# DRAM blocks of 17 and 15 rows per partition, and turns of rows to match them, in a fused residual-add layer normalisation

## The chip, the cores and the metric

The kernel runs on one core of a Trainium2 chip; nothing else is run beside it. The metric is the device time of one execution in microseconds (us). Each kernel is executed several times, and the medians are compared.

Names of engines as the profile has them: PE is TensorE, DVE VectorE, ACT ScalarE, POOL GpSimd, SP SyncE. SPq is SyncE's own instruction stream, from which it issues the transfers. They go into one DMA queue, which 16 DMA engines serve. A packet is one record of the DMA trace: here the rows of one partition in one transfer (16 rows are 32 KiB), or a completion of 4 bytes. A transfer has landed when its completions have arrived.

## The reference, cut to what matters

```python
batch, seq, dim = 16, 1024, 512              # x and residual, float32
z = x + residual
mean = np.mean(z, axis=-1, keepdims=True)
var = np.var(z, axis=-1, keepdims=True)
return gamma * (z - mean) / np.sqrt(var + eps) + beta
```

There are 16384 rows of 512 floats (2 KiB), 128 rows for each of the 128 partitions. 32 MiB of x and 32 MiB of residual come in, 32 MiB go out.

## The kernel before

Two buffers stay in SBUF: `zbuf` for 64 rows per partition of x, later of output, and `rbuf` for 32 rows of residual, later of the sum. SyncE alone issues all transfers of rows, in the order of a fixed plan (`x0+8` loads x rows 0 to 7, `o0+16` stores rows 0 to 15). A transfer is put into the queue when the buffer rows that it needs are free:

```python
BLOCK = 16
PLAN = """
x0+8 r0+8 x8+8 r8+8 x16+16 r16+16 x32+16 r32+16 x48+16
o0+16 r48+16 o16+16 x64+16 r64+16 x80+16 o32+16 r80+16
x96+16 r96+16 o48+8 o56+8 r112+8 x112+8 r120+8 x120+8
o64+16 o80+16 o96+16 o112+8 o120+4 o124+4
"""
TURN = 4
# ...
def dram(t, lo, n):            # a block of 16 rows is contiguous for a partition
    b0 = lo - lo % BLOCK
    v = t[P * b0 : P * (b0 + BLOCK), :].rearrange("(p j) d -> p j d", p=P)
    return v[:, lo - b0 : lo - b0 + n, :].rearrange("p a b -> p (a b)")
# ...
elif kind == "r":              # the residual rows' old contents must have been used
    if lo + n > R_ROWS:
        last = (lo + n - R_ROWS) // TURN - 1
        nc.sync.wait_ge(s_rstd[last % Z_TURNS], last // Z_TURNS + 1)
    move(part(rbuf, R_ROWS, lo, n), dram(rf, lo, n), sr[loads_r.index((lo, n))])
else:                          # a store waits for its rows
    if lo + n > seen:
        nc.sync.wait_ge(s_out, lo + n)
```

I call such a wait a **gate**. Compute goes in turns of four rows: GpSimd adds x into `rbuf` for the whole turn; ScalarE runs one pass for the means, one for the squares, and a square root; VectorE subtracts the mean and multiplies by gamma, takes the reciprocal (at which the turn's rows of `rbuf` are free), and scales and adds beta. Activations write to scrap tiles, since only their row sums are wanted:

```python
junk_m = [nc.alloc_psum_tensor(f"junk_m{i}", [P, D], FP32) for i in range(TURN)]
junk_s = [nc.alloc_psum_tensor(f"junk_s{i}", [P, D], FP32) for i in range(6 - TURN)]
junk_s += [nc.alloc_sbuf_tensor(f"junk_s{i}", [P, D], FP32) for i in range(6 - TURN, TURN)]
```

## Time and profile before

| | before |
|---|---|
| time, median of the first 6 runs | 238.26 us (238.23 to 238.43) |
| span of the profiled run (first to last instruction) | 236.7 us |
| transfers' share of 16 DMA engines' span | 99.4% |
| busiest compute engine | ScalarE, 78% |
| bytes moved for rows | 100.66 MB |

Read it from the bottom up: every engine that computes is idle for a fifth of the span or more, and the transfers for next to nothing. The prediction below shows the lines.

### The profile page before, as it was taken

To read this page: it belongs to the slowest core of one execution; us is meant where nothing else is said; L and a number is where in the kernel's file an instruction comes from. 1 tells how busy PE (TensorE), PEld (TensorE's weight loads), DVE (VectorE), ACT (ScalarE), POOL (GpSimd) and SP (SyncE) were. 2 spreads that over 40 slices of the span, in tenths; PEclk is the share of its full clock that TensorE was granted. 3 is DMA by queue.
4 is the path that set the end of the run, shared out by engine and by line. 5 is a ranking of instruction groups with operands and counts; after the bars stand their busy time and mean duration, and the time that the engine had idled before them with its cause. 6 is when DMAs were issued, how large, how long until landed. Compare 5 with 4: busy or idle time off the path is not lost.

```text
span 236.7 us, 1000 instructions
## 1 busy us (share of the span) xinstructions
PE 3.8 (2%) x4; PEld 1.2 (0%) x4; DVE 177.2 (75%) x290; ACT 183.8 (78%) x545; POOL 144.0 (61%) x36
## 2 busy tenths in 40 slices
PE   0600000000000000000000000000000000000000
PEld 0100000000000000000000000000000000000000
DVE  0001999629999999599980999809999999999950
ACT  2019997299999996999909998099999999999600
POOL 0098920999799307993079920899799798800000
DMA  8999999999999999999999999999999999999997
GB/s 310 443 426 432 426 443 443 443 443 443 410 388 443 443 443 432 426 393 432 443 443 443 443 438 421 415 421 432 429 424 435 426 432 440 439 432 443 438 390 324
DMA packets 4469, 100.68 MB, mean 425 GB/s; under 512 B 498, under 2 KB 498, under 8 KB 500
## 3 DMA queue, kind: packets, MB, share of 16 engines
q1 hardware_dynamic: 4464, 100.67, 99.4%
q14 instruction: 1, 0.01, 0.0%
q10 hardware_dynamic: 4, 0.00, 0.0%
HBM read 67.11 MB, written 33.55 MB: 425 GB/s over the span
## 4 chain that ended last, share of the span: by engine, by line
ACT 48%; DMA 35%; POOL 6%; DVE 4%; issue 1%; SPq 1%; ACTq 0%; DVEq 0%; POOLq 0%
DMA rbuf<-in_residual_dram 35%; ACT junk_s L211 25%; ACT junk_m L201 21%; POOL rbuf L178 6%; DVE zbuf L239 3%; ACT std L220 2%; DVE zbuf L253 1%; SPq L140 1%; DVE rstd L247 0%; ACTq L194 0%; DVEq L231 0%; POOLq L175 0%; ACTq L199 0%; ACTq L195 0%
## 5 line engine op out<-in xcount | busy, mean ns | idle before, releaser
L178 POOL TENSOR_TENSOR rbuf<-zbuf,rbuf 128x2048 f32<-128x2048 f32 x32 | 143.7, 4521 | 62.2 <-DMA rbuf<-in_residual_dram 60.0
L239 DVE SCALAR_TENSOR_TENSOR zbuf<-rbuf,nm,gamma_p 128x512 f32<-128x512 f32 x128 | 87.1, 743 | 47.8 <-ACT std L220 47.8
L201 ACT ACTIVATE junk_m<-rbuf 128x512 f32<-128x512 f32 x128 | 74.2, 580 | 34.0 <-POOL rbuf L178 33.7
L211 ACT ACTIVATE junk_s<-rbuf,nm 128x512 f32<-128x512 f32 x128 | 88.8, 694 | 1.0
L253 DVE SCALAR_TENSOR_TENSOR zbuf<-zbuf,rstd,beta_p 128x512 f32<-128x512 f32 x128 | 87.1, 744 | 1.1
L211 ACT ACTIVATION_READ_ACCUMULATOR junk_s<-rbuf,nm 128x1 f32 x128 | 23.9, 187 | 0.0
L201 ACT ACTIVATION_READ_ACCUMULATOR junk_m<-rbuf 128x1 f32 x128 | 23.8, 186 | 0.0
L220 ACT ACTIVATE std<-ssq,eps_t 128x4 f32<-128x4 f32 x32 | 9.5, 297 | 1.0
L247 DVE RECIPROCAL rstd<-std 128x4 f32<-128x4 f32 x32 | 5.5, 171 | 0.0
L192 ACT ACT_TABLE_LOAD x1 | 1.3, 1283 | 2.7 <-PEq L60 2.7
L131 PE MATMUL gamma_p<-gb_row,ones 1*128 1x512 f32 x2 | 2.0, 1122 | 6.6 <-DMA gb_row<-in_gamma_dram 6.6
L131 PE MATMUL beta_p<-gb_row,ones 1*128 1x512 f32 x2 | 1.9, 1056 | 0.0
L126 DVE MEMSET ones<- 1x128 f32 x1 | 0.2, 165 | 2.0 <-PEq L60 2.0
L131 PEld LDWEIGHTS beta_p<-gb_row,ones 1*128 1x128 f32 x2 | 0.7, 332 | 1.0 <-DMA gb_row<-in_beta_dram 0.5
L131 PEld LDWEIGHTS gamma_p<-gb_row,ones 1*128 1x128 f32 x2 | 0.5, 306 | 6.6 <-issue 6.6
L294 POOL MEMSET const-float32-0.0<- 128x1 f32 x1 | 0.1, 98 | 0.2 <-issue 0.2
L294 POOL MEMSET const-bfloat16-1.0<- 128x1 bf16 x1 | 0.1, 101 | 0.0
L294 POOL MEMSET const-uint8-127<- 128x1 uint8 x1 | 0.1, 101 | 0.0
L294 POOL MEMSET const-float32-1.0<- 128x1 f32 x1 | 0.1, 98 | 0.0
L127 DVE MEMSET eps_t<- 128x1 f32 x1 | 0.1, 59 | 0.0
## 6 DMA issues: line engine op xcount, KB each, us to landing
zbuf<-in_x_dram SPq DMA_DIRECT2D x6, 4096.0 KB, 28.9
rbuf<-in_residual_dram SPq DMA_DIRECT2D x6, 4096.0 KB, 21.2
out_dram<-zbuf SPq DMA_DIRECT2D x6, 4096.0 KB, 31.0
zbuf<-in_x_dram SPq DMA_DIRECT2D x4, 2048.0 KB, 14.9
rbuf<-in_residual_dram SPq DMA_DIRECT2D x4, 2048.0 KB, 14.0
out_dram<-zbuf SPq DMA_DIRECT2D x3, 2048.0 KB, 22.5
out_dram<-zbuf SPq DMA_DIRECT2D x2, 1024.0 KB, 10.0
gb_row<-in_gamma_dram ACTq DMA_DIRECT2D x1, 2.0 KB
```

The source lines that it names most:

```text
L126: nc.vector.memset(ones[:, :], 1.0).then_inc(s_const, 1)
L131: nc.tensor.matmul(dest[:, :], ones[:, :], gb_row[:, k * D : (k + 1) * D], start=True, stop=True).then_inc(s_pe, 1)
L140: i = nc.sync.dma_start(out=out, in_=in_).then_inc(s, 16)
L178: nc.gpsimd.tensor_tensor(out=z, in0=part(zbuf, Z_ROWS, lo, n), in1=z, op=ALU.add).then_inc(s_sum[lo // TURN % R_TURNS], 1)
L192: act.preload_act_table_set("sqrt_and_others")
L201: i = act.activation(out=junk_m[k][:, :], in_=part(rbuf, R_ROWS, r, 1), func=ACT.Identity, scale=-inv_d, accum_out=column(nm, r),)
L211: i = act.activation(out=junk_s[k][:, :], in_=part(rbuf, R_ROWS, r, 1), func=ACT.Square, bias=column(nm, r), accum_out=column(ssq, r),)
L220: act.activation(out=column(std, rows[0], TURN), in_=column(ssq, rows[0], TURN), func=ACT.Sqrt, bias=eps_t[:, 0:1], scale=inv_d,).then_inc ...
L239: dve.scalar_tensor_tensor(out=part(zbuf, Z_ROWS, r, 1), in0=part(rbuf, R_ROWS, r, 1), scalar=column(nm, r), in1=gamma_p[:, :], op0=ALU.ad ...
L247: dve.reciprocal(out=column(rstd, rows[0], TURN), in_=column(std, rows[0], TURN)).then_inc(s_rstd[j], 1)
L253: i = dve.scalar_tensor_tensor(out=z, in0=z, scalar=column(rstd, r), in1=beta_p[:, :], op0=ALU.mult, op1=ALU.add,)
L294: nc = _bacc.Bacc("TRN2", target_bir_lowering=False, num_devices=1)
```

## The change

The intent is a distance between partitions in DRAM (the pitch) that is no power of two: 17 rows are 34 KiB and 15 rows 30 KiB, where 16 are 32 KiB. The compute turns change along with it, so that a turn ends where a block does (4 + 4 + 4 + 5 = 17, 4 + 4 + 4 + 3 = 15). The core of the diff:

```diff
-BLOCK = 16
+BLOCKS = [17, 15]
 PLAN = """
-x0+8 r0+8 x8+8 r8+8 x16+16 r16+16 x32+16 r32+16 x48+16
-o0+16 r48+16 o16+16 x64+16 r64+16 x80+16 o32+16 r80+16
-x96+16 r96+16 o48+8 o56+8 r112+8 x112+8 r120+8 x120+8
-o64+16 o80+16 o96+16 o112+8 o120+4 o124+4
+x0+8 r0+8 x8+9 r8+9 x17+15 r17+15 x32+17 r32+17 x49+15
+o0+17 r49+15 o17+15 x64+17 r64+17 x81+15 o32+17 r81+15
+x96+17 r96+17 o49+7 o56+8 r113+7 x113+7 r120+8 x120+8
+o64+17 o81+15 o96+17 o113+7 o120+4 o124+4
 """
-ADDS = [4] * 32
-TURN = 4
+TURNS = [4, 4, 4, 5, 4, 4, 4, 3]
 ...
-        b0 = lo - lo % BLOCK
-        v = t[P * b0 : P * (b0 + BLOCK), :].rearrange("(p j) d -> p j d", p=P)
+        k = spot(blocks, lo)
+        b0, b1 = blocks[k], blocks[k + 1]
+        v = t[P * b0 : P * b1, :].rearrange("(p j) d -> p j d", p=P)
 ...
-    junk_m = [nc.alloc_psum_tensor(f"junk_m{i}", [P, D], FP32) for i in range(TURN)]
-    junk_s = [nc.alloc_psum_tensor(f"junk_s{i}", [P, D], FP32) for i in range(6 - TURN)]
+    junk_m = [nc.alloc_psum_tensor(f"junk_m{i}", [P, D], FP32) for i in range(most)]
+    junk_s = [nc.alloc_psum_tensor(f"junk_s{i}", [P, D], FP32) for i in range(6 - most)]
 ...
-                last = (lo + n - R_ROWS) // TURN - 1
+                last = spot(marks, lo + n - R_ROWS - 1)
 ...
-                nc.sync.wait_ge(s_out, lo + n)
+                seen = next(m for m in marks if m >= lo + n)
+                nc.sync.wait_ge(s_out, seen)
```

`marks` are the rows at which turns end, `blocks` those at which blocks begin, `spot` finds the turn or block of a row, and `most` is 5. What is left out follows from these (the loops of the engines run over `marks`).

More of the change, by code (lines that the diff above doesn't have):

```diff
@@ L19 @@
 PLAN = """
-x0+8 r0+8 x8+8 r8+8 x16+16 r16+16 x32+16 r32+16 x48+16
-o0+16 r48+16 o16+16 x64+16 r64+16 x80+16 o32+16 r80+16
-x96+16 r96+16 o48+8 o56+8 r112+8 x112+8 r120+8 x120+8
-o64+16 o80+16 o96+16 o112+8 o120+4 o124+4
-"""
-ADDS = [4] * 32
-TURN = 4
-R_TURNS = R_ROWS // TURN
-Z_TURNS = Z_ROWS // TURN
+x0+8 r0+8 x8+9 r8+9 x17+15 r17+15 x32+17 r32+17 x49+15
+o0+17 r49+15 o17+15 x64+17 r64+17 x81+15 o32+17 r81+15
+x96+17 r96+17 o49+7 o56+8 r113+7 x113+7 r120+8 x120+8
+o64+17 o81+15 o96+17 o113+7 o120+4 o124+4
+"""
+TURNS = [4, 4, 4, 5, 4, 4, 4, 3]
 EARLY = 2
@@ L56, with edges, spot @@
     total = N // P
+    def edges(sizes, end):
+        found, k = [0], 0
+        while found[-1] < end:
+            found.append(found[-1] + sizes[k % len(sizes)])
+            k += 1
+        assert found[-1] == end
+        return found
+    def spot(marks, row):
+        return max(k for k, m in enumerate(marks) if m <= row)
+    blocks = edges(BLOCKS, total)
+    marks = edges(TURNS, total)
+    most = max(TURNS)
+    r_turns, z_turns = spot(marks, R_ROWS), spot(marks, Z_ROWS)
+    assert marks[r_turns] == R_ROWS and marks[z_turns] == Z_ROWS
+    assert z_turns == 2 * r_turns
     tc.close()
@@ L64 @@
         kind, (lo, n) = word[0], map(int, word[1:].split("+"))
-        assert lo // BLOCK == (lo + n - 1) // BLOCK
+        assert spot(blocks, lo) == spot(blocks, lo + n - 1)
         moves.append((kind, lo, n))
@@ L88 @@
     beta_p = nc.alloc_psum_tensor("beta_p", [P, D], FP32)
-    junk_m = [nc.alloc_psum_tensor(f"junk_m{i}", [P, D], FP32) for i in range(TURN)]
-    junk_s = [nc.alloc_psum_tensor(f"junk_s{i}", [P, D], FP32) for i in range(6 - TURN)]
+    junk_m = [nc.alloc_psum_tensor(f"junk_m{i}", [P, D], FP32) for i in range(most)]
+    junk_s = [nc.alloc_psum_tensor(f"junk_s{i}", [P, D], FP32) for i in range(6 - most)]
     junk_s += [
-        nc.alloc_sbuf_tensor(f"junk_s{i}", [P, D], FP32) for i in range(6 - TURN, TURN)
+        nc.alloc_sbuf_tensor(f"junk_s{i}", [P, D], FP32) for i in range(6 - most, most)
     ]
@@ L108 @@
     s_sum, s_mean, s_ssq, s_std = (
-        [sem(f"{name}{j}") for j in range(R_TURNS)] for name in ("sum", "mean", "ssq", "std")
+        [sem(f"{name}{j}") for j in range(r_turns)] for name in ("sum", "mean", "ssq", "std")
     )
-    s_rstd = [sem(f"rstd{j}") for j in range(Z_TURNS)]
+    s_rstd = [sem(f"rstd{j}") for j in range(z_turns)]
     s_out = sem("out")
@@ L152 @@
             if lo + n > R_ROWS:
-                last = (lo + n - R_ROWS) // TURN - 1
-                nc.sync.wait_ge(s_rstd[last % Z_TURNS], last // Z_TURNS + 1)
+                last = spot(marks, lo + n - R_ROWS - 1)
+                nc.sync.wait_ge(s_rstd[last % z_turns], last // z_turns + 1)
             move(part(rbuf, R_ROWS, lo, n), dram(rf, lo, n), sr[loads_r.index((lo, n))])
@@ L157 @@
             if lo + n > seen:
-                nc.sync.wait_ge(s_out, lo + n)
-                seen = lo + n
+                seen = next(m for m in marks if m >= lo + n)
+                nc.sync.wait_ge(s_out, seen)
             move(dram(of, lo, n), part(zbuf, Z_ROWS, lo, n), so[stores.index((lo, n))])
@@ L170 @@
     landed = {"x": 0, "r": 0}
-    lo = 0
-    for n in ADDS:
+    for k in range(len(marks) - 1):
+        lo, n = marks[k], marks[k + 1] - marks[k]
         for key, loads, s in (("x", loads_x, sx), ("r", loads_r, sr)):
@@ L179 @@
             out=z, in0=part(zbuf, Z_ROWS, lo, n), in1=z, op=ALU.add
-        ).then_inc(s_sum[lo // TURN % R_TURNS], 1)
-        lo += n
-    assert lo == total
+        ).then_inc(s_sum[k % r_turns], 1)
     def column(t, lo, n=1):
@@ L196 @@
         due = act.snap(lap + 1)
-        for j in range(R_TURNS):
-            rows = range(j * TURN, (j + 1) * TURN)
+        for j in range(r_turns):
+            rows = range(marks[j], marks[j + 1])
             act.wait_ge(s_sum[j], due)
@@ L220 @@
             act.activation(
-                out=column(std, rows[0], TURN),
-                in_=column(ssq, rows[0], TURN),
+                out=column(std, rows[0], len(rows)),
+                in_=column(ssq, rows[0], len(rows)),
                 func=ACT.Sqrt,
@@ L234 @@
         turn = dve.snap(lap + 1)
-        for j in range(Z_TURNS):
-            rows = range(j * TURN, (j + 1) * TURN)
-            dve.wait_ge(s_std[j % R_TURNS], due[j // R_TURNS])
+        for j in range(z_turns):
+            rows = range(marks[j], marks[j + 1])
+            dve.wait_ge(s_std[j % r_turns], due[j // r_turns])
             for r in rows:
@@ L247 @@
             dve.reciprocal(
-                out=column(rstd, rows[0], TURN), in_=column(std, rows[0], TURN)
+                out=column(rstd, rows[0], len(rows)), in_=column(std, rows[0], len(rows))
             ).then_inc(s_rstd[j], 1)
@@ L260 @@
                 )
-            i.then_inc(s_out, TURN)
+            i.then_inc(s_out, len(rows))
     loops = [b for b in nc.main_func.blocks if b.name.endswith("_loop")]
```

## The prediction

> **What bounds the kernel now.** I read the page from the top, and the first part already says that no compute engine fills the span:
>
> ```profile
> span 236.7 us, 1000 instructions
> PE 3.8 (2%) x4; PEld 1.2 (0%) x4; DVE 177.2 (75%) x290; ACT 183.8 (78%) x545; POOL 144.0 (61%) x36
> ```
>
> ScalarE is busiest with 78%, so 53 us are idle on the busiest engine. The third part shows what does fill the span:
>
> ```profile
> q1 hardware_dynamic: 4464, 100.67, 99.4%
> HBM read 67.11 MB, written 33.55 MB: 425 GB/s over the span
> ```
>
> One queue carries everything, and its packets fill 99.4% of what 16 DMA engines have. 0.994 x 236.7 = 235.2 us of transfer time per engine leaves 1.5 us. The packet records put that rest at one place: the first packet starts 1.53 us after the first issue, and 1.53 + 235.16 = 236.7. So the DMA engines never wait between the first and the last packet. The measured 238.26 is this span plus some 1.5 us outside it (the profiled run took 238.0 for a span of 236.7).
>
> The chain of waits and the wait list name something else, and they are a trap here:
>
> ```profile
> ACT 48%; DMA 35%; POOL 6%; DVE 4%; issue 1%; SPq 1%; ACTq 0%; DVEq 0%; POOLq 0%
> ...
> POOL rbuf L178 <- DMA rbuf<-in_residual_dram: 60.0, 8, 11.9
> DVE zbuf L239 <- ACT std L220: 47.8, 32, 20.5
> ...
> SPq L140 <- DVE rstd L247: 131.6, 7, 38.5
> SPq L140 <- DVE zbuf L253: 50.6, 7, 22.9
> ```
>
> GpSimd waits 60 us for residual rows, that is, compute waits for data. SyncE waits 131.6 us for VectorE before it may issue loads, and the chain follows those waits. They would matter only if the queue ran dry meanwhile. The windows that I cut at the chain's turning points show that it doesn't (columns: window, us, busy time per engine, clock, DMA share, GB/s):
>
> ```profile
> 12.30:41.40 29.10, 0.00 (x0) 0.00 (x0) 18.06 (x30) 22.83 (x68) 17.96 (x4) 1.00 1.01 436
> ...
> 119.40:148.70 29.30, 0.00 (x0) 0.00 (x0) 22.29 (x38) 22.82 (x68) 17.94 (x4) 1.00 1.00 429
> 148.70:222.60 73.90, 0.00 (x0) 0.00 (x0) 64.93 (x106) 68.37 (x204) 53.95 (x12) 1.00 1.01 433
> ```
>
> The DMA share is 1.00 or 1.01 in each. From each transfer's issue and the landing of the one before it in the queue I worked out how much work lay queued at each issue. After the start the least is 5.8 us, at the last store (issued at 228.23, the one before lands at 234.07). The next are 8.23 us (the residual load of rows 96 to 111, issued at 150.08) and 8.31 us (rows 32 to 47, at 42.77). **The bound is the rate at which 16 DMA engines move 100.66 MB.**
>
> **How near that rate is to its floor.** The packet records by size: 2304 packets of 32 KiB, least 1213 ns, median 1216; 1408 of 16 KiB, least 611, median 611; 256 of 8 KiB, least and median 309; 496 of 4 bytes (completions) of 9 ns. Two of these give a line: (1213 - 611) / 16 KiB = 602 ns for 16 KiB, and 9 ns per packet; 8 KiB then gives 310, measured 309. 16 engines x 16384 B / 602 ns = 435.5 GB/s. Every packet at its least: (2304 x 1213 + 1408 x 611 + 256 x 309 + 496 x 9) / 16 = 233.66 us. The excess is 235.16 - 233.66 = 1.50 us. Of this, 0.68 us is the first packets of the run (each engine's first 16 KiB takes 1020 to 1368 ns), and 0.43 us one event at 69.0 to 69.4 us, where each of the 16 engines has one 32 KiB packet of 1316 to 1908 ns, about when the first store reaches the engines. What is left is 0.4 us in the whole run.
>
> **What the Trainium skill says.**
> 1. "DMA: Bandwidth & Descriptors", section "Where 436 GB/s comes from", gives 16 ports x 32 B x 850 MHz = 435.2 GB/s as the ceiling. The trace agrees: 435.5 GB/s from the slope of the packet times.
> 2. "HBM Reference", section "Specifications (TRN2)": a core that streams alone reaches about 425 GB/s, bounded by its 16 DMA engines rather than HBM. The trace has 425 GB/s over the span.
> 3. "DMA: Bandwidth & Descriptors", section "Latency and other measured facts", row "HBM row pitch at large powers of two": a pitch of 512 KiB and above can cut a copy's rate, and padding the pitch by 4 KiB restored full rate at 4 MiB. This is the argument for the change: a block of 16 rows has a pitch of 32 KiB between partitions, one of 17 has 34 KiB, one of 15 has 30. But 32 KiB lies far under the pitches listed, and in this trace the packets at that pitch have their median 3 ns over their least. The loss that the change could cure isn't there.
> 4. The same page, section "How a descriptor splits into AXI transactions": a descriptor aligned to 256 B becomes transactions of 256 B without a rest. 34 and 30 KiB rows of 2 KiB keep that, so odd blocks should cost nothing there.
>
> **The change part by part.**
> *Packets.* The plan keeps its 31 moves: 10 of x, 10 of the residual, 11 stores, in the same queue order. Each is still 128 runs, so there are the same 3968 data packets, 496 completions and bytes. By the line above a 34 KiB packet takes 9 + 17/8 x 602 = 1288 ns and a 30 KiB one 9 + 15/8 x 602 = 1138 ns; their mean is 1213, what 32 KiB takes. Floor unchanged at 233.66 us: **0**.
> *Pitch.* At most the 0.4 us of scattered excess can go; the 0.68 and 0.43 us strike the first packet of each engine and one packet of each engine, so they look tied to the event and not to an address. I book **-0.1**.
> *Turns.* Rows per lap and instructions per row are the same: 32 adds, 128 of each activation, 32 square roots. A turn of 5 or 3 rows only moves work. Since marks 17 and 32 coincide with block ends, each load still waits for just the turn that frees its rows, except the 7-row residual load, which waits for a turn that ends one row further, and two of the last stores, which wait for the turn ending at 121 and at 125 where they need 120 and 124.
> *Timing of gates.* One row costs ScalarE about 1.4 us (a turn of four is 2.46 + 2.94 + 0.30 + gaps = 5.75) and one row of transfer 0.60 us. For a 17-row gate: its data land up to 1.2 us later, ScalarE has one more row (1.4), VectorE one more (0.7), while the queue ahead is longer by up to 1.2. The load at 150.08 would come some 3.3 us later into a queue that is 1.2 us longer: 8.23 - 2.1 = 6.1 us of backlog. That at 42.77: some 6.8. 15-row gates come earlier. At the end, the last chain starts with row 81 instead of 80, 0.6 us later with one row less, so ScalarE ends about 0.8 us sooner, and the last turn has three rows, which VectorE finishes some 1.4 us faster. The last store is then issued near 226 instead of 228.2, the two before it about 1.4 us nearer to their queue's end than now (9.1 and 10.0 us of backlog). Nothing runs dry: **0**.
> *Scrap buffers.* Five mean-pass scrap tiles take five PSUM banks, leaving one for the squares, whose other four tiles lie in SBUF (two and two now). In the timeline a square into PSUM took 0.69 and 0.67 us, into SBUF 0.71, and successive ones start 0.70 to 0.72 us apart either way. Even +0.02 us on the roughly 40 moved ones is 0.8 us over the whole of an engine with 53 us of slack: **0**.
> Sum: 238.26 - 0.1 = 238.2 us.
>
> **The rivals.**
> *The odd pitch spreads addresses and speeds HBM.* For it: the pitch of 32 KiB is a power of two. Against it: packets at their least take the same time per byte at every size, and the median sits on the least. Even with all excess gone it is 238.3 - 1.5 = 236.8 us, 0.6% faster.
> *A gate runs dry.* A 5-row turn delays a release, the queue empties and the DMA share falls under 1. The least backlog that I get is some 6 us, so my gate estimates would have to be wrong by more than twice. If one did, some 1 to 3 us: 239 to 241.
> *Larger packets are slower than the line says,* for instance because a run over 32 KiB is split. No packet over 32 KiB is in this trace. If each 34 KiB run became two packets, the cost is some 9 ns on about 1150 packets over 16 engines: 0.7 us, 238.9. If the odd pitch met a conflict that the even one avoids, 2% of all packets' time would be 5 us, 243.
>
> **Range and chances.** The centre is 238.2. The runs before spread over 0.2 us. Downwards, half of the excess going is 237.5; upwards, split packets or a small stall give 239.0. So 237.5 to 239.0. Faster by over 2% needs a time under 233.5, which asks for a span of 232, below the floor of 233.66: 1%. Slower by over 2% needs 243.0, a conflict or a badly failed gate: 2%. Within 2%: 97%.
>
> **What would show it right or wrong.** Right: the queue again at 99% or more with 4464 packets, 34 KiB packets near 1288 ns and 30 KiB ones near 1138, DMA share 1.0 in the inner windows, ScalarE and VectorE totals within a microsecond of 183.8 and 177.2, the last store issued near 226 and the slow packets at the run's start still there. It is wrong if inner windows fall below a share of 0.98 (a gate ran dry), if the packet count rises (runs are split), or if packet times leave the line (HBM or the engines care about the pitch).

Slips in it, none of which changes its sum:

- The 32 KiB packets' 1216 ns is their upper quartile. Their median is 1213, equal to the least, which makes the same point more strongly.
- Its times of packets are 0.5 us late. Counted from the first issue, the first packet starts at 1.02 us, not 1.53, and the last one ends 0.52 us before the span does: the 1.5 us without transfers lie at both ends. The group of slow packets starts at 68.5 to 68.9 us. The first packets' excess comes out at 0.62 us instead of 0.68.
- A third store waits for more rows than it needs: that of rows 49 to 55 waits for the turn ending at 57. It was issued at 153.74, right behind the load before it, so this cost nothing.
- The scrap buffers move 32 squares to SBUF (24 of every 32 instead of 16), not roughly 40.

## The result, and the profile after

The changed kernel took **238.42 us** (median of 6 runs, 238.06 to 239.03), the kernel before 238.26 us. The ratio is 1.0009, with a 95% interval of 0.9994 to 1.0025: the same.

From the page of the changed kernel, its span, its compute engines and its one busy queue (packets, MB, share of 16 engines):

```profile
span 236.7 us, 1000 instructions
...
PE 3.7 (2%) x4; PEld 1.2 (0%) x4; DVE 176.6 (75%) x290; ACT 183.8 (78%) x545; POOL 144.0 (61%) x36
...
q1 hardware_dynamic: 4464, 100.67, 99.3%
```

As many packets, as many bytes, as full a queue, as much ScalarE. The packet records have a median of 1288 ns for the 1280 packets of 34 KiB and 1138 ns for the 1024 of 30 KiB, to the nanosecond what the line through the old sizes gave. The transfer time of one engine adds up to 235.14 us (235.16 before): 233.63 with every packet at the least of its size, and 1.51 in excess (1.50 before). I set aside two odd 16 KiB packets that took less than 611 ns (608 the least); with 608 as the least, the excess would read 1.63. In what follows, too, the least of a size is the one below which only a few odd packets fall: 611, 1138, 1213, 1288 ns.

The chain that ended last, by engine, and what SyncE waited for (engine and line, what it waited for, us in total, times, longest):

```profile
DMA 37%; ACT 34%; DVE 18%; POOL 6%; issue 1%; SPq 1%; ACTq 0%; DVEq 0%; POOLq 0%
...
SPq L154 <- DVE rstd L259: 127.1, 7, 40.6
SPq L154 <- DVE zbuf L265: 50.5, 7, 25.8
```

The chain looks quite different: VectorE's share went from 4% to 18%, ScalarE's from 48% to 34%. The time didn't move. On the page this suggests that the chain of waits doesn't bound this kernel: it follows the gates, and behind every gate work still lies queued. Run 8 tests it. The windows of the changed kernel (window, us, busy time per engine, clock, DMA share, GB/s) keep a share of 1.0 inside:

```profile
12.30:41.40 29.10, 0.00 (x0) 0.00 (x0) 16.63 (x28) 24.15 (x72) 19.06 (x4) 1.00 1.02 437
...
119.40:148.70 29.30, 0.00 (x0) 0.00 (x0) 19.93 (x33) 23.06 (x70) 19.02 (x4) 1.00 1.01 435
148.70:222.60 73.90, 0.00 (x0) 0.00 (x0) 66.25 (x109) 68.16 (x204) 52.87 (x12) 1.00 1.00 431
```

The work queued at each issue (landing of the transfer before it, less its own issue) is never under 6.2 us after the start: 6.92 us at the residual load of row 32 on (issued 44.87), 6.28 us at that of row 96 on (153.37), 6.22 us at the last store (227.93). The first two of these issues as the timeline of SyncE has them (start, us, what):

```profile
44.87 0.33 SPq L154 DMA_DIRECT2D rbuf<-in_residual_dram  x1
...
153.37 0.33 SPq L154 DMA_DIRECT2D rbuf<-in_residual_dram  x1
```

Counted up to the landing, this overstates the slack by some 1.5 us: the run's last packet ends 0.5 us before its landing, and into an empty queue the first packet starts 1.0 us after the issue (at the start of the run).

What did change a little is the scatter of the times, 1.0 us over six runs against 0.2 us. The experiments take this up.

### The profile page after: what moved, and what is told of

Same layout as the page of the kernel before. It is cut to its first block, busy times and chain, and to the rows that moved or that the text cites. A ratio compares the mean times of both kernels' runs of the same rounds, so it can differ in the third digit from the quotient of the medians.

```text
span 236.7 us, 1000 instructions
## 1 busy us (share of the span) xinstructions
PE 3.7 (2%) x4; PEld 1.2 (0%) x4; DVE 176.6 (75%) x290; ACT 183.8 (78%) x545; POOL 144.0 (61%) x36
## 3 DMA queue, kind: packets, MB, share of 16 engines
q1 hardware_dynamic: 4464, 100.67, 99.3%
## 4 chain that ended last, share of the span: by engine, by line
DMA 37%; ACT 34%; DVE 18%; POOL 6%; issue 1%; SPq 1%; ACTq 0%; DVEq 0%; POOLq 0%
DMA rbuf<-in_residual_dram 37%; ACT junk_s L223 17%; ACT junk_m L213 15%; DVE zbuf L251 10%; DVE zbuf L265 8%; POOL rbuf L192 6%; ACT std L232 2%; SPq L154 1%; DVE rstd L259 0%; ACTq L206 0%; DVEq L243 0%; POOLq L189 0%; ACTq L211 0%; ACTq L207 0%
## 5 line engine op out<-in xcount | busy, mean ns | idle before, releaser
L192 POOL TENSOR_TENSOR rbuf<-zbuf,rbuf 128x2048 f32<-128x2048 f32 (+2 forms) x32 | 143.8, 4525 | 65.9 <-DMA rbuf<-in_residual_dram 61.9
L223 ACT ACTIVATE junk_s<-rbuf,nm 128x512 f32<-128x512 f32 x128 | 89.9, 703 | 1.0
L232 ACT ACTIVATE std<-ssq,eps_t 128x4 f32<-128x4 f32 (+2 forms) x32 | 9.5, 298 | 1.0
L259 DVE RECIPROCAL rstd<-std 128x4 f32<-128x4 f32 (+2 forms) x32 | 5.5, 172 | 0.0
```

What stands on the lines that cost most here:

```text
L192: nc.gpsimd.tensor_tensor(out=z, in0=part(zbuf, Z_ROWS, lo, n), in1=z, op=ALU.add).then_inc(s_sum[k % r_turns], 1)
L223: i = act.activation(out=junk_s[k][:, :], in_=part(rbuf, R_ROWS, r, 1), func=ACT.Square, bias=column(nm, r), accum_out=column(ssq, r),)
L232: act.activation(out=column(std, rows[0], len(rows)), in_=column(ssq, rows[0], len(rows)), func=ACT.Sqrt, bias=eps_t[:, 0:1], scale=inv_d, ...
L259: dve.reciprocal(out=column(rstd, rows[0], len(rows)), in_=column(std, rows[0], len(rows))).then_inc(s_rstd[j], 1)
```

## The experiments

My theory: the time is what 16 DMA engines need for these bytes; all compute and all gates are hidden behind it; the pitch of 32 KiB costs nothing, so that 34 and 30 KiB have nothing to win, and the two halves of the change are neutral only together. Rivals: the odd pitch does win time and the uneven turns eat it; the odd pitch costs scattered packets; compute and its waits hold a part of the time.

### 1. The changed kernel again

No edit.

> The changed kernel unaltered, to have it beside the next three on one chip and to see its scatter: its first six runs spread over 1.0 us (238.06 to 239.03), those of the kernel before over 0.2 us. My theory (the rate of the DMA engines binds, pitch and turns cost nothing): ratio to before between 0.999 and 1.003, 238.1 to 239.0 us. Rival (the odd pitch costs scattered packets): the same wide scatter again, with some runs near 239.

Measured: 238.81 us (238.28 to 239.12, 6 runs), the kernel before 238.19 us on the same chip (238.06 to 239.24, 11 runs), ratio 1.0008 (0.9988 to 1.0028). So the result repeats, and with more runs the kernel before reaches 239.24 as well: long executions aren't the change's alone. Whether they come more often with it, these few runs don't tell.

This run's profile fell into one of the longer executions (239.12 us, span 237.8). Set it beside that of the first profile of the same kernel (238.06, 236.7): the packet records show what the scatter looks like. An engine's last packet is a completion of 4 bytes. Counted from the first packet, the 16 last completions end on average at 234.54 us in the shorter execution and the latest at 235.21; in the longer one the average is 234.84 and the latest 236.39. The average moved by 0.3 us and the latest by 1.2 us: one DMA engine fell behind, and the run ends with the last. Why one engine falls behind in some executions, the records don't tell, since they don't name the engine.

### 2. The pitch alone, at 64 KiB

```diff
-BLOCKS = [17, 15]
+BLOCKS = [32]
```

> The changed kernel with its moves of 17 and 15 rows and its turns kept, but blocks of 32 rows in DRAM: the pitch between partitions is 64 KiB, a power of two. It separates the pitch from everything else in the change. My theory: 238.2 to 238.6 us, the same as the changed kernel within 0.2%. Rival 1 (the odd pitch speeds DRAM, and the turns eat that gain): slower than the changed kernel by 0.5 us or more. Rival 2 (the odd pitch costs scattered packets): 238.2, and a scatter of 0.2 us as before, without runs near 239.

Measured: 238.65 us (238.32 to 238.97), ratio 1.0006 (0.9988 to 1.0024), against 1.0008 for the changed kernel in the same rounds. Same moves, same turns, a pitch that is a power of two: the same time. To within these intervals of 0.2% the odd pitch neither wins nor loses here, so the first two rivals fall: there was no gain for the turns to eat. The packet records are less even. The profiled execution has 236.07 us of transfer time per engine against 235.53 in run 1, and 58 of its 1024 packets of 30 KiB take over 1.08 times their least, against 41. These are single profiles, and the times show nothing of it; whether 64 KiB begins to cost something stays open.

### 3 and 4. The pitch alone, at 256 KiB

The changed kernel with one block, and the kernel before with one block:

```diff
-BLOCKS = [17, 15]
+BLOCKS = [128]
```

> As the run with a pitch of 64 KiB, with one block of 128 rows: pitch 256 KiB, close under the 512 KiB at which the Trainium skill's page DMA: Bandwidth & Descriptors (section Latency and other measured facts) lists the first loss. My theory: 238.2 to 238.8 us, packets of 34 KiB still at a median of 1288 to 1292 ns. A pitch effect would show here first: over 240 us, and medians over 1320 ns.

```diff
-BLOCK = 16
+BLOCK = 128
```

> The kernel before with one block of 128 rows: pitch 256 KiB in place of 32, same 16-row moves and turns of four. My theory: 238.2 to 238.6 us, ratio within 0.2% of 1. If a power-of-two pitch costs anything in this kernel, it is more here than at 32 KiB: over 240 us.

Measured: 240.40 us (240.04 to 240.65), ratio 1.0083 (1.0064 to 1.0102), and 240.52 us (239.90 to 240.74), ratio 1.0082 (1.0062 to 1.0101). Here my expectation was wrong: the pitch does matter once it is large enough. It isn't the bulk of the packets: in the packet records the median of a 34 KiB packet is 1288 ns and that of a 32 KiB one 1213, as without the large pitch. It is single slow packets: 71 of the 1024 packets of 30 KiB take over 1.08 times their least in the first of these runs, 41 in run 1. The excess over the least times is 2.74 and 3.24 us, against 1.90 us in run 1. The latest engine ends 1.6 and 1.8 us after the average, but so it does in run 1 (1.6), so that isn't the pitch's. The idea behind the change is thus not baseless. It starts from a pitch, 32 KiB, at which there is nothing to cure.

### 5. A pitch near 256 KiB that is no power of two

```diff
-BLOCKS = [17, 15]
+BLOCKS = [113, 15]
```

> The changed kernel with DRAM blocks of 113 and 15 rows: the pitch is 226 KiB for the first 113 of 128 rows, near 256 KiB but no power of two; moves and turns as in the changed kernel. The pitch of 256 KiB cost 0.8% (240.4 us). If it was the power of two, this run is back at 238.3 to 238.9 us. If it was the size of the pitch alone (partitions far apart in DRAM), it stays at 239.8 to 240.6 us.

Measured: 239.26 us (238.07 to 239.82), ratio 1.0030 (1.0009 to 1.0051), beside 238.43 us of the kernel before. This lies between the two expectations. Leaving the power of two took off most of the loss (0.3% instead of 0.8%), but the scatter is as large as what is left, and the runs at 256 KiB come from other rounds. The rest need not be the distance's: run 8, which has the pitches of 34 and 30 KiB and comes from the same chip and the same kernel before, reads 1.0026. The packet records of the profiled execution are those of run 1: 235.49 us of transfer time per engine (235.53 there), 40 slow packets of 30 KiB (41). They show no cost of the distance alone; the times don't settle it.

### 6. The turns alone

```diff
-BLOCKS = [17, 15]
+BLOCKS = [16]
 # and the plan of the kernel before
```

> The turns of 4, 4, 4, 5, 4, 4, 4, 3 with the blocks and moves of 16 rows of the kernel before. By my account of the gates it runs the queue dry twice: the residual load of row 32 on frees rows 0 to 15, but must now wait for the turn of rows 13 to 16, whose last row comes with the residual load landing at 41.4. From there 4.5 us of adds, 5.75 of ScalarE, 2.9 of VectorE and 1.5 to the first packet: 56.1, while the queue ends at 51.1: 5 us dry. The same at row 96 (waits for row 80, landing at 148.6): 4.9 us. Expected 248 us, 246 to 250, DMA share well under 1 in windows near 51 to 56 and 163 to 168. Rival (gates have slack to spare, turns cost nothing in any case): 238 to 239 us.

Measured: 261.27 us (260.64 to 261.94, 4 runs), ratio 1.0971 (1.0953 to 1.0989). The direction and both gates are as expected, the size is over twice mine (some 23 us over the kernel before, where I expected 10). Windows of this run, around the two gates:

```profile
51.30:58.00 6.70, 0.00 (x0) 0.00 (x0) 3.48 (x6) 6.63 (x21) 6.70 (x3) 1.00 0.00 0
58.00:60.50 2.50, 0.00 (x0) 0.00 (x0) 2.47 (x4) 2.47 (x8) 2.50 (x1) 1.00 0.73 210
60.50:70.20 9.70, 0.00 (x0) 0.00 (x0) 9.63 (x17) 9.60 (x30) 3.60 (x2) 1.00 1.00 432
...
171.00:177.70 6.70, 0.00 (x0) 0.00 (x0) 3.48 (x6) 6.64 (x21) 6.70 (x3) 1.00 0.00 0
177.70:180.20 2.50, 0.00 (x0) 0.00 (x0) 2.46 (x5) 2.47 (x8) 2.50 (x1) 1.00 0.77 210
```

The DMA share is 0.00 for 6.7 us, twice. (A packet is counted in the window in which it starts.) The timelines of the engines show the gate opening: landing, the adds, the square root of the turn of five, VectorE's reciprocal, and only then the issue of the residual load (start, us, engine, line, operation; the rest of the lines as in the page).

```profile
54.18 0.30 ACT L232 ACTIVATE std<-ssq,eps_t 128x5 f32<-128x5 f32 x1
...
57.81 0.18 DVE L259 RECIPROCAL rstd<-std 128x5 f32<-128x5 f32 x1
...
58.02 0.33 SPq L154 DMA_DIRECT2D rbuf<-in_residual_dram  x1
```

My sum for this gate had used a turn of four; the turn that ends at row 17 has five rows, so adds, activations and VectorE end at 58.0 rather than 54.6. And restarting a dry queue takes longer than the 1.5 us that I allowed: the load issued at 58.02 lands at 70.17, and its packets alone take 8 x 1.213 = 9.7 us, which leaves 2.4 us. The packet records show where it goes: the first packet starts 0.96 us after the issue, each engine's first packet takes 1.25 to 2.15 us where the least is 1.21, and the landing follows the last packet by some 0.4 us (as at the end of this run). The span less the transfer time per engine, that is the time without a packet, is 19.9 us against 1.5 in the kernel before, 18.4 more. The transfer time is 239.38 us instead of 235.16, 4.2 more. Together these are the 22.6 us by which the span grew (259.3 - 236.7). Of the 4.2 us, 1.3 are the first packets after the two restarts. Most of the rest are groups of slow packets in the last loads before stores follow in the queue (around 78, 137 and 188 us), a larger form of the group near 69 us in the kernel before. I expected none of this, and why they grow stays open.

### 7. The blocks alone

```diff
-TURNS = [4, 4, 4, 5, 4, 4, 4, 3]
+TURNS = [4]
```

> The blocks and moves of 17 and 15 rows with turns of four throughout. The residual load of row 32 on frees rows 0 to 16, and row 16 belongs to the turn of rows 16 to 19, whose other rows land at 41.5: 41.5 + 4.5 + 5.75 + 2.9 + 1.5 = 56.1, while the queue ends at 51.8: 4.3 us dry. The same at row 96 (turn of rows 80 to 83, landing at 149.3): 4.3 us. Expected 247 us, 245 to 249. Rival (slack to spare): 238 to 239 us. A gain from the odd pitch would have to show as less than this.

Measured: 251.99 us (251.67 to 252.04, 4 runs), ratio 1.0568 (1.0553 to 1.0583). The same mechanism from the other side: row 16 now lies in a turn whose other three rows come with the next load. The windows of this run:

```profile
51.80:54.90 3.10, 0.00 (x0) 0.00 (x0) 2.81 (x5) 3.07 (x10) 3.10 (x1) 1.00 0.00 0
54.90:57.40 2.50, 0.00 (x0) 0.00 (x0) 2.48 (x4) 2.50 (x8) 2.50 (x2) 1.00 0.78 223
...
167.00:170.10 3.10, 0.00 (x0) 0.00 (x0) 2.81 (x5) 3.07 (x10) 3.10 (x1) 1.00 0.00 0
170.10:173.00 2.90, 0.00 (x0) 0.00 (x0) 2.72 (x4) 2.87 (x10) 2.90 (x2) 1.00 0.69 192
```

The gates open at 54.9 and 170.1, 3.1 us after the queue has run out, as worked out (41.5 + 4.5 + 5.75 + 2.9 = 54.7). The size is again larger for the restart: from issue to landing 12.93 us for 10.3 us of packets at the first, 14.12 at the second. The records have 11.0 us per engine without a packet more than the changed kernel, and 2.9 us more transfer time; together these are the 13.9 us by which the span grew (250.66 against 236.73).

Runs 6 and 7 together: each half of the change alone costs 14 to 23 us, and together they cost nothing. They also show that the gates are no formality. The gate that opens at 44.87 in the changed kernel is free, the same gate opening at 54.91 costs over 5 us.

### 8. The transfers without the compute

Wrong (relative error 0.77, as the output is x). The compute engines' code goes, and the gates wait for landings:

```diff
-                last = spot(marks, lo + n - R_ROWS - 1)
-                nc.sync.wait_ge(s_rstd[last % z_turns], last // z_turns + 1)
+                while loads_r[old][0] < lo + n - R_ROWS:
+                    nc.sync.wait_ge(sr[old], 16)
+                    old += 1
 ...
-                seen = next(m for m in marks if m >= lo + n)
-                nc.sync.wait_ge(s_out, seen)
+            while seen < len(loads_x) and loads_x[seen][0] < lo + n:
+                nc.sync.wait_ge(sx[seen], 16)
+                seen += 1
 ... the code of GpSimd, ScalarE and VectorE for the rows is left out
```

> Wrong on purpose: the moves of the changed kernel without its compute. The output is x; stores wait for the loads of x, residual loads for the residual loads whose rows they overwrite. My theory (the rate of the 16 DMA engines sets the time and all compute is hidden): 238.0 to 238.9 us, the same as the whole kernel within 0.3%. Rival (compute and its waits set some of the time, as the chain suggests): clearly less, under 236 us.

Measured: 238.79 us (238.38 to 239.63, 4 runs), ratio to the kernel before 1.0026 (1.0005 to 1.0047). Its page:

```profile
PE 3.7 (2%) x4; PEld 1.2 (0%) x4; DVE 0.2 (0%) x2; POOL 0.2 (0%) x4
...
q1 hardware_dynamic: 4464, 100.67, 99.3%
```

No row is computed, the queue is 99.3% full again, and the time is no shorter. The last rival falls: compute and its waits hold no part of the 238 us that could be seen here. So rearranging compute has nothing to win in this plan of transfers, and no run pointed to a version that would beat both.

## Why the prediction was right

**The bound.** That the queue binds, and not the chain, is shown by run 8, and from the other side by runs 6 and 7, where the share fell to 0.00 and the time rose. Whether the DMA engines or the memory behind them set the least time of a packet, no run here separates; the prediction's second point on this rests on the page it names and not on a run.

**Packets: 0.** Right: 4464 packets, medians of 1288 and 1138 ns as the line gave. Nothing was split.

**Pitch: -0.1.** Right within what can be measured: the excess was 1.51 us instead of 1.50, and run 2, which changes the pitch alone (to 64 KiB), finds no difference in time. The slow first packets are still there in the changed kernel (947 to 1538 ns for twelve of the 16 engines' first packets, whose least is 608), and so is the group of slow packets shortly before the first store's turn. What the prediction had not foreseen is that a pitch below the skill's list can cost something: 256 KiB does (runs 3 and 4); 64 KiB shows nothing in the time.

**Timing of gates: 0.** Right, and close: 6.1 us of backlog predicted and 6.28 measured at row 96, 6.8 and 6.92 at row 32. One term was mis-sized. The last store was to be issued near 226 and was at 227.93. I had let VectorE's end follow ScalarE's, with a last turn that VectorE finishes 1.4 us faster. But the turn of five rows takes VectorE 6.9 us (3.38 + 0.11 + 3.38 in the chain), against 5.7 us for ScalarE's next turn, one of four rows, so it fell behind there and ran back to back to the end. It cost nothing because 6.22 us of stores still lay queued.

**Scrap buffers: 0.** The mean of a square went from 694 to 703 ns, 128 x 9 ns = 1.1 us of summed durations (0.8 estimated), and ScalarE's busy time stayed at 183.8 us, since successive activations overlap: in the kernel before, the durations of ScalarE's instructions add up to some 222 us, its busy time to 183.8.

**Rivals.** A gain from the pitch was given 1.5 us at most, from the excess; none came. The dry gate was given 1 to 3 us. In the changed kernel no gate ran dry; but where one did (runs 6 and 7) it cost more, 5.7 to 10.2 us each (landing to landing, less the transfer's own packets), which I would now put into that rival.

**Range.** The measured 238.42 lies in it. The scatter that I had taken from the first runs of the kernel before (0.2 us) was too small: with eleven runs it is 1.2 us. The range had been made wider for other risks; that it covers this scatter too is luck.

## What to carry to other kernels

When one queue is busy for 99% of the span, work out its floor from the packets' least times and the work queued at each issue; a change that alters neither bytes nor packets and leaves some microseconds queued at every gate moved nothing here, however different the chain of waits looks afterwards. Transfer sizes and compute turns belong together: a turn that reaches one row into the next load can hold up the queue for the length of that turn's whole way through the engines, and restarting the queue added 2.4 to 3.8 us in these runs. Before curing a pitch in DRAM, look whether packets at that pitch are any slower than the least.

## What the Trainium skill lacked or had wrong

- "DMA: Bandwidth & Descriptors", section "Latency and other measured facts", row "HBM row pitch at large powers of two": its list starts at 512 KiB. Here a pitch of 256 KiB already cost 0.8% (240.40 and 240.52 us against 238.19), as single slow packets; 64 KiB cost nothing that the times show (ratio 1.0006 beside 1.0008), and 226 KiB, no power of two, lay between (1.0030, interval 1.0009 to 1.0051). The page's copies are DRAM to DRAM, these are loads and stores.
- The same section gives some 600 ns to the first byte for transfers issued from SyncE. The trace agrees: at the four dry gates of runs 6 and 7 the first packet starts 0.96 to 0.98 us after the issue's start, 0.63 to 0.65 us after its end. The section has no figure for a whole transfer that restarts a dry queue, and the page's fixed cost from setup to completion is for transfers issued from GpSimd: here, from issue to landing, the loads behind these four gates took 2.4 to 3.8 us more than their own packets (12.15 - 9.7 us, and 14.12 - 10.3 us), in part because each engine's first packet is slow (1.25 to 2.15 us instead of 1.21 at the first gate).
- "ScalarE: Activation LUTs", section "Step-by-step: what each stage is for", says that writing to PSUM is faster than to SBUF. As a single duration it is (0.67 and 0.69 us against 0.71), but successive squares start 0.70 to 0.72 us apart in either case, and writing 24 of 32 of them to SBUF instead of 16 left ScalarE's busy time at 183.8 us. (Each is followed by a read of the accumulator.) That no throughput is lost isn't said there.
- No page that I used gives the scatter of a single core's saturated queue: the same kernel took 238.06 to 239.24 us over eleven runs.
